# Input projection of a hybrid encoder layer: stick-breaking transposes and heads, statistics broadcast and convolution taps at other ticks

## Chip, cores, metric

One Trainium2 chip, one of its cores. The metric is the device time of one execution in microseconds; several executions are timed and the median is given. One further execution is profiled.

## What is computed

One layer (`DEPTH = 1`) over a sequence of 1024 rows of width 1024, all in float32. The projection `u` has 3328 columns and is split over three mixers; their outputs are concatenated, projected, and followed by an MLP with a squared ReLU.

```python
h = rms_norm(x, mix_norm_g)
u = einsum('btd,dc->btc', h, w_in)
sb_q, sb_k, sb_v, r_q, r_k, r_v, r_g, c_a, c_gate = split(u)
# 1. stick-breaking attention, 4 heads of 64, q and k normalised by head
z = q.k / sqrt(64);  mask: key < query
w = exp(log_sigmoid(z) + reverse_cumsum(log_sigmoid(-z), shifted));  y_sb = w @ v
# 2. retention, 8 heads of 64: rotary(q), rotary(k), decayed causal scores,
#    then rms_norm by head and silu(r_g) * ret
# 3. conformer convolution, 256 channels: (a + b) * sigmoid(gate + b),
#    31 causal depthwise taps, layer_norm over channels, silu
x = x + concat([y_sb, y_ret, y_conv]) @ w_out
x = x + relu(rms_norm(x) @ w_ff1)**2 @ w_ff2
```

## The kernel before

All float32 products are made of three passes: each operand is split into a high part (cast on ACT, lines 181 and 769) and a remainder (subtracted on DVE or POOL, lines 182 and 770), and `mm3` (lines 118 to 120) multiplies high by high, low by high and high by low.

**Order of the work.** The code is written out without loops on the chip. The input projection runs group by group of weight columns (`GROUPS`); each half of a tile (four of the eight 128-row pieces of the contraction) is one *tick*. `at_tick(t, order, fn)` hangs other work on a tick, and `tick` emits it, by `order`, ahead of that tick's matmuls. What is emitted is then arranged by a scheduler that works with a cost model of its own: the tick sets a priority and no fixed place, so an engine's instructions can stand earlier or later than their tick. Each engine then runs its own list strictly in order. In `conv_taps` a group of taps is tied behind an *anchor*, the latest evacuation of a projection tile on DVE (line 561 or 726).

**Ticks.** The first group (q and k of head pair 0, and all v) runs ahead of tick 0, over all eight PSUM banks. Ticks 0 to 15 are the group "qk1" (q and k of head pair 1, tiles of 256 columns, `gemm_narrow`); its tiles go into the two banks of tag "g" in turn, and a tile's bank comes free when `qk1_evac` has normalised it (`sb_norm`, lines 288 to 300). Ticks 16 to 31 are the convolution's two halves, gated by `conv_gate` (lines 498 to 509), which needs `rbc`, the row statistic broadcast over partitions (`row_bcast`, lines 249 to 256). Ticks 32 to 95 are the four wide retention groups, ticks 96 to 111 the first part of the output projection (`out_job(0, dt)`, three of eight contraction pieces); then `out_job(1, dt)` adds the other five.

**Stick-breaking.** `sb_norm` normalises a tile of q and k into `qn`, in a tile of tag "cv", of which there are two; two row tiles share one. `sb_turn` transposes four row tiles (lines 305 and 306) and splits them into `qs`, `ka`, `kb` (lines 314 to 321: per call 4 plus 2 ACT and 6 DVE operations). A head is 12 steps, four heads 48 steps; a step's `a_step` makes scores (lines 348 to 351, banks "z"), two sigmoids, a product scan on DVE (line 361) and a product on POOL (line 365); `b_step` transposes the weights two ticks later (line 376) and splits them (378, 379); `c_step` multiplies with v after each pair of steps (395).

**Pair 0 before the change.** `norm0(range(4))` runs ahead of tick 0; `turn0(0)` at tick 1 is followed by `norm0(range(4, 8))`, since both "cv" tiles are in use until the transposes; `turn0(1)` at tick 3. The 48 steps start at ticks 2 to 49. `row_bcast` is emitted at tick 16, with its own two "cv" tiles.

**Convolution.** 124 taps (line 588 for the first of a channel tile, 591 for the others; 31 taps, two channel tiles, two halves of the sequence, the second half first) run on DVE at ticks 35 to 99, `per` of them at a tick. A half's two `conv_norm_a` (transposes 601, statistics 606 to 608, scaling 612) and `conv_norm_b` (transposes 621, lines 626 to 629) follow; the results are split by `split_mixed(4)` and `split_mixed(5)` for `out_job(1, dt)`.

Of the kernel before, what the change touches and what calls it, by code (L numbers as in the profile page):

```python
# [15 lines left out]
P = 128  # L16
# [3 lines left out]
NT = T // P  # L20
# [58 lines left out]
def build(tc, d):  # L79
# [27 lines left out]
    def slot(tag, shape=(P, T), dt=F32):  # L107
        pool = xp if tag[0] == "x" else pg
        return pool.tile(list(shape), dt, tag=tag, name=nm(tag + "_"))

    def page(i, shape=(P, T), dt=F32):
        return slot(f"P{i}", shape, dt)

    def small(tag, shape, bufs=2, dt=F32):
        return sm.tile(list(shape), dt, tag=tag, name=nm(tag), bufs=bufs)
# [133 lines left out]
    def row_bcast(out, col, tag, by="cv"):  # L249
        for hf in range(2):  # L250
            ps = bank(tag)
            dg = small(by, (P, 4, P))
            V.tensor_tensor(out=dg, in0=ident.unsqueeze(1).to_broadcast([P, 4, P]),
                            in1=col[:, 4 * hf:4 * hf + 4].unsqueeze(2).to_broadcast([P, 4, P]), op=ALU.mult)
            TE.matmul(ps, ones, dg.rearrange("p a b -> p (a b)"), start=True, stop=True)
            S.copy(out[:, 512 * hf:512 * hf + 512], ps)
# [7 lines left out]
    def at_tick(t, order, fn):  # L264
        steps.setdefault(t, []).append((order, len(steps.get(t, [])), fn))
# [21 lines left out]
    def sb_norm(pair, tt, src):  # L287
        sq = small("e1", (P, 256))
        S.activation(sq, src, AF.Square)
        ss = small("ss", (P, 4))  # L290
        V.tensor_reduce(out=ss, in_=sq.rearrange("p (a b) -> p a b", b=DH), axis=AX.X, op=ALU.add)
        V.tensor_scalar(out=ss, in0=ss, scalar1=1.0 / DH, scalar2=ceps[:, tt:tt + 1], op0=ALU.mult, op1=ALU.add)
        rs = small("rs", (P, 4))
        rpow(rs, ss)
        if tt % 2 == 0:
            tb[tt // 2] = small("cv", (P, 2, 256))
        qn = tb[tt // 2][:, tt % 2, :]
        V.tensor_tensor(out=qn.rearrange("p (a b) -> p a b", b=DH), in0=src.rearrange("p (a b) -> p a b", b=DH),
                        in1=rs.unsqueeze(2).to_broadcast([P, 4, DH]), op=ALU.mult)

    def sb_turn(pair, tg):
        pq, pk = bank("t"), bank("t")
        for u in range(4):
            qn = tb[2 * tg + u // 2][:, u % 2, :]
            TE.transpose(pq[:, u * P:u * P + P], qn[:, 0:P], ident)
            TE.transpose(pk[:, u * P:u * P + P], qn[:, P:2 * P], ident)
        ts = slice(tg * 512, tg * 512 + 512)
        t = hd[pair]
        for e in range(2):
            a = slice(64 * e, 64 * e + 64)  # L310
            b = slice(64 * (1 - e), 64 * (1 - e) + 64)
            gq, gk = vec[a, V_GQ:V_GQ + 1], vec[a, V_GK:V_GK + 1]
            qs, ka, kb = t["qs", e], t["ka", e], t["kb", e]
            S.activation(qs[a, ts], pq[a, :], AF.Copy, scale=gq)
            V.scalar_tensor_tensor(out=qs[b, ts], in0=pq[a, :], scalar=gq, in1=qs[a, ts].bitcast(F32),  # L315
                                   op0=ALU.mult, op1=ALU.subtract)
            S.activation(kb[a, ts], pk[a, :], AF.Copy, scale=gk)
            V.scalar_tensor_tensor(out=kb[b, ts], in0=pk[a, :], scalar=gk, in1=kb[a, ts].bitcast(F32),
                                   op0=ALU.mult, op1=ALU.subtract)
            S.copy(ka[b, ts], kb[a, ts].bitcast(F32))  # L320
            V.tensor_copy(ka[a, ts], kb[b, ts].bitcast(F32))
# [9 lines left out]

    mix_sb = {}

    def sb_head(pair, e, t0):
        h = 2 * pair + e
        tick0 = t0
        for m in range(4):
            st = {"carry": {}, "first": True}

            def a_step(m, jg, ii, key, st):  # L340
                t = hd[pair]
                qs, ka, kb = t["qs", e], t["ka", e], t["kb", e]
                s0, i = 512 * jg, 2 * m + ii
                n = min(512, P * (i + 1) - s0)
                last = s0 + n == P * (i + 1)
                pz = bank("z")
                qt = qs[:, i * P:i * P + P]
                TE.matmul(pz[:, 0:n], qt, kb[:, s0:s0 + n], start=True, stop=False)
                if last:
                    TE.matmul(pz[:, n - P:n], identb, maskb, start=False, stop=False)  # L350
                TE.matmul(pz[:, 0:n], qt, ka[:, s0:s0 + n], start=False, stop=True)  # L351
                be = small("be", (P, 512), 3)
                kp = small("kp", (P, 513), 2)
                S.activation(kp[:, 0:n], pz[:, 0:n], AF.Sigmoid, scale=-0.125)  # L354
# [12 lines left out]

            def b_step(m, jg, ii, key, st):
                if ii == 0:
                    st["w", jg] = page(18, (P, 4, 2, P), F32R), page(19, (P, 4, 2, P), F32R)  # L370
                wth, wtl = st["w", jg]
                be, n = st["be", jg, ii]
                nj = n // P
                pt = bank("t")
                for j in range(nj):
                    TE.transpose(pt[:, j * P:j * P + P], be[:, j * P:j * P + P], ident)  # L376
                src = pt[:, 0:n].rearrange("p (j c) -> p j c", c=P)
                S.copy(wth[:, 0:nj, ii, :], src)
                V.tensor_tensor(out=wtl[:, 0:nj, ii, :], in0=src, in1=wth[:, 0:nj, ii, :].bitcast(F32),
                                op=ALU.subtract)  # L380
# [22 lines left out]

            for jg in range((2 * m + 1) // 4, -1, -1):
                for ii in range(2):
                    at_tick(t0, 30, lambda a=(m, jg, ii, None, st): a_step(*a))
                    at_tick(t0 + 2, 20, lambda a=(m, jg, ii, None, st): b_step(*a))
                    t0 += 1
                at_tick(t0 + 2, 10, lambda a=(m, jg, None, st): c_step(*a))
        return t0  # L410

    def parts(n, lo_engine=None):
# [54 lines left out]
    def norm0(tts):  # L467
        for tt in tts:
            sb_norm(0, tt, raw0[tt // 2][:, tt % 2, 0:256])

    def turn0(tg):
        sb_turn(0, tg)
        if tg == 0:
            norm0(range(4, 8))

    norm0(range(4))
    for tt in range(NT):
        v_evac(tt, raw0[tt // 2][:, tt % 2, 256:512])
    at_tick(1, 5, lambda: turn0(0))
    at_tick(3, 5, lambda: turn0(1))  # L480
    t1 = sb_head(0, 0, 2)
    t1 = sb_head(0, 1, t1)
    t1 = sb_head(1, 0, t1)
    sb_end = sb_head(1, 1, t1) + 4
    mix_sb[1] = page(17)
    sb_prepare(1)

# [3 lines left out]
            at_tick(now[0] + 1, 5, lambda: sb_turn(1, tt // 4))  # L491

    gemm_narrow(qk1_evac)
    rbc = slot("DM")
    at_tick(now[0], 6, lambda: row_bcast(rbc, rstd, "o"))
    glu = [None, None]

    def conv_gate(ct, hf, pa, pgt):
# [131 lines left out]

    c0 = 35
    taps = [(ct, hf, j) for hf in (1, 0) for j in range(TAPS) for ct in range(2)]
    per = [1] * 22 + [2] * 7 + [3] * 16 + [2] * 20
    n, t = 0, c0
    while n < len(taps):
        at_tick(t, 40, lambda a=taps[n:n + per[t - c0]]: conv_taps(a))
        n, t = n + per[t - c0], t + 1
    for t2, t in ((2, 81), (3, 85), (0, 100), (1, 102)):
        at_tick(t, 25, lambda t2=t2: conv_norm_a(t2))
        at_tick(t + 2, 25, lambda t2=t2: conv_norm_b(t2))  # L640

# [212 lines left out]
    def out_proj(pi, dt, hf):  # L854
        tsl = slice(512 * hf, 512 * hf + 512)
        w = taken[pi, dt]
        ps = bank("o" if pi else "g")
        for k in w:
            mm3(ps, w[k][0], w[k][1], mh[k][:, tsl], ml[k][:, tsl], k == min(w), k == max(w))
        V.tensor_tensor(out=x2[dt][:, tsl], in0=ps, in1=x2[dt][:, tsl], op=ALU.add)  # L860

    jobs = [(pi, dt) for pi in range(2) for dt in range(NK)]
# [329 lines left out]
```

## Time and profile before

| | us |
|---|---|
| median of 3 runs (1157.25 to 1157.94) | 1157.6 |
| the profiled execution, its own time | 1159.54 |
| its span, first to last instruction | 1157.8 |
| TensorE (PE) busy in the span | 1121.4 (97%) |
| VectorE (DVE) busy | 897.7 (78%) |
| ScalarE (ACT) busy | 484.1 (42%) |
| GpSimd (POOL) busy | 519.1 (45%) |
| mean granted TensorE clock, as a share of 2.4 GHz | 0.992 |

PE is the engine with the least idle time, so the time is read from the places where PE is idle or runs at the lower clock, and from what ended each idle time. The view of windows gives by stretch the busy time of each engine, with the number of instructions, and the granted clock; the view of waits says which instruction of which engine ended the idle time before an instruction; the timeline lists instructions in order of time.

### The profile page before, as it was taken

The numbers are of one execution on the slowest core, as the hardware profiler recorded it, in microseconds if no ns is written. First come the engines' busy times: TensorE is split into PE (matmuls) and PEld (weight loads), VectorE is DVE, ScalarE is ACT, GpSimd is POOL, SyncE is SP. The second block draws the span as 40 slices with busy tenths as digits, with TensorE's granted clock in tenths as the row PEclk, the third lists the DMA queues.
The fourth block names the chain that finished last, engine by engine and source line by source line (L and its number), as shares of the span: only waits on it lengthen the run. The fifth ranks groups of instructions, "written<-read, shape, count | busy, mean of one in ns | idle before, by whom it ended". The sixth has DMA issues, their size and how long they took to land.

```text
span 1157.8 us, 15678 instructions
## 1 busy us (share of the span) xinstructions
PE 1121.4 (97%) x5416; PEld 933.0 (81%) x5416; DVE 897.7 (78%) x1378; ACT 484.1 (42%) x917; POOL 519.1 (45%) x413
## 2 busy tenths in 40 slices
PE   8968899999999989999999999999999999999997
PEld 6857788888887878888888888888878788888886
DVE  7498677787899898579975666666699897886963
ACT  7366655453322242356433333333443443444441
POOL 4356234473555463242466565655583531522300
PEclk9989999999999989999999999999999999999999
DMA  8101011030202051112254444444787464552342
GB/s 277 48 1 46 19 42 55 19 110 15 87 24 87 20 217 61 55 73 91 78 187 148 152 161 140 164 146 141 279 304 264 130 219 129 164 182 82 110 136 73
DMA packets 63727, 137.00 MB, mean 118 GB/s; under 512 B 7200, under 2 KB 11936, under 8 KB 63648
## 3 DMA queue, kind: packets, MB, share of 16 engines
q1 hardware_dynamic: 63072, 135.56, 35.3%
q8 instruction: 43, 0.70, 0.3%
q10 hardware_dynamic: 576, 0.44, 0.1%
q14 instruction: 36, 0.29, 0.1%
HBM read 98.22 MB, written 37.75 MB: 117 GB/s over the span
## 4 chain that ended last, share of the span: by engine, by line
PE 47%; DVE 5%; issue 3%; POOL 2%; ACT 0%; DVEq 0%; POOLq 0%; ACTq 0%
PE g L119 4%; PE g L120 4%; PE g L118 4%; PE t L119 4%; PE t L118 4%; PE t L120 4%; PE o L119 4%; PE o L120 4%; PE o L118 4%; PE z L119 4%; PE z L118 4%; PE z L120 4%; DVE wlo L182 1%; POOL sum L903 1%; POOL wr L903 0%
## 5 line engine op out<-in xcount | busy, mean ns | idle before, releaser
L182 DVE TENSOR_TENSOR wlo<-sum,whi 128x512 fp32r<-128x512 f32 x78 | 80.2, 1029 | 84.2 <-ACT whi L181 84.1
L181 ACT CAST whi<-sum 128x512 fp32r<-128x512 f32 x78 | 47.9, 617 | 101.4 <-POOL sum L903 50.9
L182 DVE TENSOR_TENSOR wlo<-wr,whi 128x512 fp32r<-128x512 f32 x80 | 76.4, 960 | 6.9 <-ACT whi L181 6.9
L908 POOL TENSOR_TENSOR sum<-wr 128x512 f32<-128x512 f32 x16 | 23.4, 1466 | 120.2 <-DMA wr<-in_w_ff_dram 92.7
L365 POOL TENSOR_TENSOR be<-be,kp 128x512 f32<-128x512 f32 (+3 forms) x48 | 44.6, 932 | 70.5 <-DVE kp L361 33.1
L181 ACT CAST whi<-wr 128x512 fp32r<-128x512 f32 x80 | 48.2, 620 | 51.7 <-PE t L119 17.6
L196 POOL TENSOR_TENSOR rs<-ss,nhalf 128x4 f32<-128x4 f32 (+1 forms) x36 | 36.8, 1024 | 66.8 <-DVE ss L699 44.7
L361 DVE TENSOR_TENSOR_SCAN kp<-kp 128x512 f32<-128x512 f32 (+3 forms) x48 | 53.4, 1118 | 10.1 <-ACT kp L354 9.8
L591 DVE SCALAR_TENSOR_TENSOR DM__439_2052<-glu,vec,DM__439_2052 128x512 f32<-128x512 f32 x60 | 52.7, 921 | 0.0
L591 DVE SCALAR_TENSOR_TENSOR glu<-glu,vec 128x512 f32<-128x512 f32 x60 | 50.3, 881 | 0.0
L354 ACT ACTIVATE kp<-z 128x512 f32<-128x512 f32 (+3 forms) x48 | 23.7, 493 | 36.2 <-PE z L351 22.0
L182 POOL TENSOR_TENSOR wlo<-wraw,whi 128x512 fp32r<-128x512 f32 x18 | 28.4, 1585 | 22.6 <-ACT whi L181 21.2
L903 POOL TENSOR_TENSOR sum<-wr,sum 128x512 f32<-128x512 f32 x19 | 32.8, 1725 | 9.9 <-DVE wlo L182 9.9
L903 POOL TENSOR_TENSOR sum<-sum,wr 128x512 f32<-128x512 f32 x18 | 24.4, 1357 | 12.5 <-DVE wlo L182 12.5
L376 PE MATMUL t<-ident,be 128*128 128x128 f32 x144 | 25.1, 276 | 4.2 <-DVE P__108_534 L315 1.6
L181 ACT CAST whi<-wraw 128x512 fp32r<-128x512 f32 x33 | 20.1, 619 | 19.5 <-PE g L119 10.0
L563 POOL TENSOR_TENSOR P__538_2584<-P__397_1882 128x128 f32<-128x128 f32 x16 | 14.5, 906 | 29.0 <-DVE P__397_1882 L561 29.0
L182 POOL TENSOR_TENSOR wlo<-rawq,whi 128x512 fp32r<-128x512 f32 x14 | 23.7, 1699 | 7.8 <-ACT whi L181 7.5
L355 ACT ACTIVATE be<-z 128x512 f32<-128x512 f32 (+3 forms) x48 | 23.7, 493 | 8.4 <-PE t L376 8.4
L376 PEld LDWEIGHTS t<-ident,be 128*128 128x128 f32 x144 | 16.9, 140 | 8.1 <-issue 5.7
L903 POOL TENSOR_TENSOR wr<-wr,wr 128x512 f32<-128x512 f32 x16 | 22.5, 1406 | 1.1
L681 ACT ACTIVATE e<-o 128x256 f32<-128x256 f32 x16 | 6.2, 385 | 38.6 <-PE o L679 37.9
(2941 smaller groups left out, 4141.6 us busy)
## 6 DMA issues: line engine op xcount, KB each, us to landing
wr<-in_w_ff_dram SPq DMA_DIRECT2D x40, 512.0 KB, 3.9
wraw<-in_w_in_dram SPq DMA_DIRECT2D x32, 256.0 KB, 2.7
rawq<-in_w_in_dram SPq DMA_DIRECT2D x20, 256.0 KB, 2.8
P__396_1881<-in_rot_dram SPq DMA_DIRECT2D x32, 128.0 KB, 2.0
wraw<-in_w_out_dram SPq DMA_DIRECT2D x10, 256.0 KB, 2.8
rawq<-in_w_out_dram SPq DMA_DIRECT2D x6, 256.0 KB, 3.5
P__18_144<-in_xT_dram SPq DMA_DIRECT2D x1, 512.0 KB, 5.1
P__24_182<-in_xT_dram SPq DMA_DIRECT2D x1, 512.0 KB, 6.2
```

Of the source, the lines that this page charges most:

```text
L118: TE.matmul(out, lh, rh, start=start, stop=False, skip_group_check=on)
L119: TE.matmul(out, lh, rl, start=False, stop=False, skip_group_check=on)
L120: TE.matmul(out, ll, rh, start=False, stop=stop, skip_group_check=on)
L181: S.copy(hi, raw)
L182: (lo_engine or GP).tensor_tensor(out=lo, in0=raw, in1=hi.bitcast(F32), op=ALU.subtract)
L196: GP.tensor_tensor(out=out, in0=in_, in1=nhalf[:, 0:in_.shape[1]], op=ALU.pow)
L354: S.activation(kp[:, 0:n], pz[:, 0:n], AF.Sigmoid, scale=-0.125)
L361: V.tensor_tensor_scan(rev, rev, rev, kp[:, n:n + 1], op0=ALU.mult, op1=ALU.bypass)
L365: GP.tensor_tensor(out=be[:, 0:n], in0=be[:, 0:n], in1=kp[:, 1:n + 1], op=ALU.mult)
L376: TE.transpose(pt[:, j * P:j * P + P], be[:, j * P:j * P + P], ident)
L591: V.scalar_tensor_tensor(out=acc, in0=src, scalar=vec[:, o:o + 1], in1=acc, op0=ALU.mult, op1=ALU.add)
L903: (eng or GP).tensor_tensor(out=o, in0=x, in1=y, op=ALU.subtract)
```

## The change

Six things are altered, all of them order or storage; every product, tap and norm stays.

1. `norm0` runs for all eight row tiles ahead of tick 0; its results lie in pages 19 and 10 and no longer in "cv" tiles. `turn0(0)` moves from tick 1 to 3, `turn0(1)` from 3 to 6.
2. The 48 steps start at the ticks of `sb_ticks`: ten steps at ticks 6 to 15, twenty at ticks 16 to 30 (two at each third tick), the rest from tick 31.
3. `row_bcast` for `rbc` is emitted ahead of tick 0, with pages 10 and 11 for its operand.
4. Taps by tick: 15 ticks of one (35 to 49), 14 of two (50 to 63), 16 of three (64 to 79), 16 of one and two in turn (80 to 95), nine of one (96 to 104).
5. The norms of the second half go from ticks 81 and 85 to 72 and 76, those of the first half from 100 and 102 to 105 and 107 (`conv_norm_b` two ticks later each).
6. `split_mixed(4)` is emitted with `split_mixed(5)` after the seventh output job and no longer after the sixth, and `out_job(1, dt)` takes its pieces in the order 3, 6, 7, 4, 5.

```diff
-            dg = small(by, (P, 4, P))
+            dg = small(by, (P, 4, P)) if by else page(10 + hf, (P, 4, P))
...
         if tt % 2 == 0:
-            tb[tt // 2] = small("cv", (P, 2, 256))
-        qn = tb[tt // 2][:, tt % 2, :]
+            if pair == 0:
+                tb[0, tt // 2] = nrm0[tt // 4][:, tt % 4:tt % 4 + 2, :]
+            else:
+                tb[1, tt // 2] = small("cv", (P, 2, 256))
+        qn = tb[pair, tt // 2][:, tt % 2, :]
...
+    sb_ticks = list(range(6, 16)) + [16 + 3 * (i // 4) + (0, 0, 1, 2)[i % 4] for i in range(20)] + list(range(31, 60))
...
-                    at_tick(t0, 30, lambda a=(m, jg, ii, None, st): a_step(*a))
-                    at_tick(t0 + 2, 20, lambda a=(m, jg, ii, None, st): b_step(*a))
+                    at_tick(sb_ticks[t0], 30, lambda a=(m, jg, ii, None, st): a_step(*a))
+                    at_tick(sb_ticks[t0] + 2, 20, lambda a=(m, jg, ii, None, st): b_step(*a))
...
-        if tg == 0:
-            norm0(range(4, 8))
-
-    norm0(range(4))
+
+    rbc = slot("DM")
+    row_bcast(rbc, rstd, "o", None)
+    nrm0 = [page(19, (P, 4, 256)), page(10, (P, 4, 256))]
+    norm0(range(NT))
...
-    at_tick(1, 5, lambda: turn0(0))
-    at_tick(3, 5, lambda: turn0(1))
-    t1 = sb_head(0, 0, 2)
+    at_tick(3, 5, lambda: turn0(0))
+    at_tick(6, 5, lambda: turn0(1))
+    t1 = sb_head(0, 0, 0)
...
-    rbc = slot("DM")
-    at_tick(now[0], 6, lambda: row_bcast(rbc, rstd, "o"))
...
-    per = [1] * 22 + [2] * 7 + [3] * 16 + [2] * 20
+    per = [1] * 15 + [2] * 14 + [3] * 16 + [1, 2] * 8 + [1] * 9
...
-    for t2, t in ((2, 81), (3, 85), (0, 100), (1, 102)):
+    for t2, t in ((2, 72), (3, 76), (0, 105), (1, 107)):
...
-        for k in w:
-            mm3(ps, w[k][0], w[k][1], mh[k][:, tsl], ml[k][:, tsl], k == min(w), k == max(w))
+        ks = (3, 6, 7, 4, 5) if pi else tuple(w)
+        for k in ks:
+            mm3(ps, w[k][0], w[k][1], mh[k][:, tsl], ml[k][:, tsl], k == ks[0], k == ks[-1])
...
-        if dt in (1, 5, 6):
-            split_mixed({1: 3, 5: 4, 6: 5}[dt])
+        if dt == 1:
+            split_mixed(3)
+        if dt == 6:
+            split_mixed(4)
+            split_mixed(5)
```

## Rows read from the trace of the kernel before

**Rows 1.** Windows by stage: length, each engine's busy us (xinstructions), PE clock, DMA share, GB/s.

```profile
57.70:72.23 14.53, 7.23 (x31) 5.12 (x30) 13.77 (x38) 10.59 (x23) 8.49 (x9) 0.69 0.00 0
72.23:104.79 32.56, 27.45 (x211) 25.53 (x209) 28.35 (x61) 21.89 (x47) 16.30 (x16) 0.98 0.02 5
104.79:178.35 73.56, 70.43 (x385) 58.14 (x386) 51.30 (x98) 40.58 (x89) 29.71 (x30) 1.00 0.16 47
...
248.49:307.79 59.30, 59.30 (x353) 51.69 (x352) 45.62 (x88) 21.12 (x53) 26.45 (x28) 1.00 0.13 43
307.79:361.11 53.32, 52.57 (x272) 44.39 (x270) 52.71 (x92) 12.05 (x29) 28.16 (x28) 1.00 0.14 45
361.11:420.00 58.89, 56.97 (x311) 47.83 (x310) 52.83 (x97) 19.26 (x46) 30.59 (x31) 1.00 0.20 64
420.00:440.00 20.00, 16.20 (x75) 13.42 (x75) 19.91 (x37) 5.16 (x13) 12.30 (x11) 0.83 0.82 315
...
480.00:500.00 20.00, 19.78 (x88) 16.04 (x87) 11.03 (x14) 8.12 (x12) 5.52 (x4) 1.00 0.24 79
```

**Rows 2.** Windows of 5 us in the first and seventh of these stages, columns as above.

```profile
65.00:70.00 5.00, 3.20 (x13) 2.69 (x14) 4.78 (x13) 4.51 (x9) 2.03 (x2) 0.50 0.00 0
...
430.00:435.00 5.00, 5.00 (x18) 4.32 (x18) 4.95 (x12) 0.75 (x2) 2.68 (x3) 0.50 1.02 401
```

**Rows 3.** Waits of PE, 50 to 110 us: total us, times, longest.

```profile
PE z L348 <- DVE P__71_449 L318: 3.5, 1, 3.5
PE t L305 <- DVE cv L298: 3.0, 3, 1.9
PE g L118 <- DVE cv L298: 2.2, 2, 1.1
```

**Rows 4.** Timeline of PE: last matmul of tick 3, first of tick 4 (start, us).

```profile
57.68 0.29 PE L120 MATMUL g<-whi,xl__59_380 128*128 128x256 f32 x1
...
72.23 0.41 PE L118 MATMUL g<-whi,xh__12_101 128*128 128x256 f32 x1
```

**Rows 5.** Timeline of DVE, the first normalisation of a tick's tile.

```profile
71.45 0.42 DVE L298 TENSOR_TENSOR cv<-g,rs 128x256 f32<-128x256 f32 x1
```

**Rows 6.** Lines of DVE, 57.7 to 104.8 us: xcount, busy us, mean ns.

```profile
L361 DVE TENSOR_TENSOR_SCAN kp<-kp 128x512 f32<-128x512 f32 (+3 forms) x11 | 11.8, 1077 | 1.8 <-ACT kp L354 1.7
```

**Rows 7.** Views of single lines: xcount, duration ns min/median/max, first and last start.

```profile
L253 DVE TENSOR_TENSOR cv<-ident,rstd x2: 694/706/719, 124.1 to 125.7; 128x512 f32<-128x512 f32 x2
...
L255 PE MATMUL o<-cv,ones x4: 592/630/697, 124.9 to 127.0; 128*128 128x512 f32 x4
...
L591 DVE SCALAR_TENSOR_TENSOR glu<-glu,vec x60: 710/742/1778, 343.2 to 443.8; 128x512 f32<-128x512 f32 x60
...
L606 DVE BATCH_NORM_STATS2 bst<-t x8: 406/418/432, 367.5 to 470.8; 128x6 f32<-128x256 f32 x8
...
L612 DVE TENSOR_SCALAR cv<-t,bmv,rs x8: 535/537/544, 373.1 to 472.9; 128x256 f32<-128x256 f32 x8
...
L628 DVE TENSOR_SCALAR e<-t,vec x8: 532/540/544, 377.7 to 479.4; 128x256 f32<-128x256 f32 x8
...
L601 PE MATMUL t<-ident,DM__439_2052 x8: 270/272/275, 349.6 to 387.2; 128*128 128x128 f32 x8
```

**Rows 8.** Line 770 on DVE, 410 to 440 us, as above.

```profile
L770 DVE TENSOR_TENSOR xl__795_4303<-P__542_2591,xh__794_4302 x2: 677/678/679, 420.3 to 422.6; 128x512 fp32r<-128x512 f32 x2
L770 DVE TENSOR_TENSOR xl__827_4465<-P__543_2592,xh__826_4464 x2: 1743/1750/1756, 423.8 to 425.5; 128x512 fp32r<-128x512 f32 x2
```

**Rows 9.** Waits of PE, 360 to 440 us: the longest.

```profile
PE o L678 <- DVE P__396_1881 L695: 3.1, 1, 3.1
```

**Rows 10.** Timeline of POOL beside the splits of rows 8.

```profile
423.71 4.61 POOL L182 TENSOR_TENSOR wlo<-wraw,whi 128x512 fp32r<-128x512 f32 x3 [1.61 <-ACT whi L181]
```

**Rows 11.** Timeline of PE: first transposes of the last norms, and the wait on their last split.

```profile
455.68 0.60 PE L601 MATMUL t<-ident,glu 128*128 128x128 f32 x4
...
483.23 0.50 PE L119 MATMUL o<-P__880_4699,whi 128*128 128x512 f32 x1 [0.22 <-DVE P__880_4699 L770]
```

More of the change, by code (lines that the diff above doesn't have):

```diff
@@ L303, in sb_turn @@
         for u in range(4):
-            qn = tb[2 * tg + u // 2][:, u % 2, :]
+            qn = tb[pair, 2 * tg + u // 2][:, u % 2, :]
             TE.transpose(pq[:, u * P:u * P + P], qn[:, 0:P], ident)
@@ L332, in build @@
     mix_sb = {}
+    sb_ticks = list(range(6, 16)) + [16 + 3 * (i // 4) + (0, 0, 1, 2)[i % 4] for i in range(20)] + list(range(31, 60))
     def sb_head(pair, e, t0):
         h = 2 * pair + e
-        tick0 = t0
         for m in range(4):
@@ L405, in sb_head @@
                 for ii in range(2):
-                    at_tick(t0, 30, lambda a=(m, jg, ii, None, st): a_step(*a))
-                    at_tick(t0 + 2, 20, lambda a=(m, jg, ii, None, st): b_step(*a))
+                    at_tick(sb_ticks[t0], 30, lambda a=(m, jg, ii, None, st): a_step(*a))
+                    at_tick(sb_ticks[t0] + 2, 20, lambda a=(m, jg, ii, None, st): b_step(*a))
                     t0 += 1
-                at_tick(t0 + 2, 10, lambda a=(m, jg, None, st): c_step(*a))
+                at_tick(sb_ticks[t0] + 2, 10, lambda a=(m, jg, None, st): c_step(*a))
         return t0
@@ L472, in turn0 @@
         sb_turn(0, tg)
-        if tg == 0:
-            norm0(range(4, 8))
-    norm0(range(4))
+    rbc = slot("DM")
+    row_bcast(rbc, rstd, "o", None)
+    nrm0 = [page(19, (P, 4, 256)), page(10, (P, 4, 256))]
+    norm0(range(NT))
     for tt in range(NT):
         v_evac(tt, raw0[tt // 2][:, tt % 2, 256:512])
-    at_tick(1, 5, lambda: turn0(0))
-    at_tick(3, 5, lambda: turn0(1))
-    t1 = sb_head(0, 0, 2)
+    at_tick(3, 5, lambda: turn0(0))
+    at_tick(6, 5, lambda: turn0(1))
+    t1 = sb_head(0, 0, 0)
     t1 = sb_head(0, 1, t1)
     t1 = sb_head(1, 0, t1)
-    sb_end = sb_head(1, 1, t1) + 4
+    sb_head(1, 1, t1)
     mix_sb[1] = page(17)
```

## The prediction

> **What bounds the kernel now.** I read the page first: PE is busy for 97% of the span, so a change of order can win only where PE is idle or runs at its lower clock. Then the windows by stage show where that is [rows 1]. Between 57.7 and 72.2 us (from the end of tick 3 to tick 4) PE is busy for 7.23 of 14.53 us, 7.3 idle; in ticks 4 to 15 for 27.45 of 32.56, 5.1 idle; in ticks 16 to 31 3.1 of 73.6 are idle; in ticks 80 to 95 1.9 of 58.9; at the passage into the output projection (420 to 440) 3.8 of 20. Beside that the granted clock falls in two places, to 0.50 of 2.4 GHz, which is its lower level of 1.2 GHz [rows 2]. At 0.69 over 14.53 us it was low for 0.31 / 0.5 x 14.53 = 9 us, at 0.83 over 20 for 6.8 us; PE was at work in an estimated 6.5 us of each (3.2 and 5.0 in the rows shown, the rest beside them), and half of that, about 3.3 us, is what each fall cost. Everything after 500 us is untouched by the change.
>
> The waits name what ended PE's idle time [rows 3]: the transposes wait for a normalised tile (3.0 us), the first scores for the split of the transposed tile (3.5), the projection for a bank that the normalisation has not yet left (2.2). The timeline shows the knot. After tick 3 both "g" banks are full; tick 4 needs the first to be normalised; that result wants a "cv" tile, and both hold pair 0 until `turn0(0)` and then `turn0(1)` have transposed them. The bank's normalisation comes at 71.45 us [rows 5], and tick 4 starts at 72.23, 14.3 us behind the end of tick 3 [rows 4].
>
> But what is DVE doing meanwhile? It is busy for 13.77 of 14.53 us, and for 28.35 of 32.56 in the next stage [rows 1]: 42.1 of 47.1, or 89%. So the knot of "cv" tiles orders a queue that is full anyway; untying it frees little unless DVE's own work leaves the stage.
>
> **The change, part by part.**
>
> *Norms into pages, transposes at ticks 3 and 6, heads from tick 6 (ticks 4 to 15).* The same normalisations and transposes run on the same engines, so they cost what they cost. What leaves the stage is four of the fourteen steps that started by tick 15. Each takes off DVE a scan of 1.08 us [rows 6], a split of a transposed tile (0.68 for 512 columns by the same kind of subtraction [rows 8], about 0.5 at a mean of 350 columns), and about 0.2 of small copies: 4 x 1.78 = 7.1 us. The broadcast enters with two products of 0.71 us [rows 7], 1.4. Net -5.7 us on the engine that sets the pace, so tick 16 comes about 5.7 us earlier, near 99 us. From below: 0, if the order of ACT or POOL takes DVE's place. From above: if every wait goes, 12.4 us idle and 3.3 of clock. I take 5.7, because the DVE share of 89% leaves only 5 us more.
>
> *Broadcast behind the first group.* PE's four pieces of 0.63 us [rows 7] now fall where PE waits for tick 4 in any case, so 2.5 us leave ticks 16 to 31. The new wait is for the row statistic, and on PE the gemm of ticks 0 to 3 or the idle time behind it is queued there; if the scheduler puts the broadcast ahead of those ticks, they merely fill the idle time later. I cost it at nothing; without that cover it would be the pieces' 2.5 us and as much for the product ahead of them.
>
> *Twenty steps instead of sixteen in ticks 16 to 31.* PE has 70.4 us of work there [rows 1]; four steps add about 0.9 each (two score products, two to four transposes, the share of `c_step`), 3.6, less the 2.5 of the broadcast: 71.5. DVE has 51.3 + 7.1 - 1.4 = 57, so it fits behind PE. Of the 3.1 us idle I leave 2: at the doubled ticks two steps want the two "z" banks and the two tiles of the scan at once. That is 73.5, as before, and the gain at tick 16 is kept: -5.7.
>
> How long a scan takes is not one number here: taps, which like it read two SBUF tensors, go from 0.71 to 1.78 us [rows 7]. The Trainium skill, "SBUF — State Buffer", section "Who interferes with whom", says that a VectorE instruction with two SBUF inputs and a GpSimd instruction that reads SBUF exclude each other, the second waiting for the whole of the first. That speaks against pushing steps closer together, since every scan is followed by a POOL product: by the rule the four moved scans could take some 4 us more on DVE. The spread in the taps agrees with it. The sum stays, as DVE has 16 us to spare in that stage.
>
> *Taps and norms of the second half (ticks 48 to 95).* Seven taps move to ticks 50 to 56, where DVE is busy for 45.6 of 59.3 us [rows 1]: covered. Ticks 80 to 95 lose eight taps of 0.74 and two pairs of norms, each 2 x (0.42 + 0.54 + 0.54) = 3.0 us on DVE [rows 7]: 11.9 of 52.8 us. PE's 1.9 us idle there should go. But the norms' 6.0 us land in ticks 72 to 79, in a stage where DVE has no room (52.7 of 53.3). The cover is the second "g" bank, two ticks or 24 matmuls of 19.78 / 88 = 0.225 us [rows 1], 5.4 us; I charge 0.5. Net -1.5, from -2.7 (the 0.8 us of ticks 64 to 79 gone as well) to +4 (all of the 6.0 on PE, less 1.9).
>
> *The passage at 420 to 440 us.* The longest wait, 3.1 us, is for line 695 [rows 9], which stood on DVE behind eight splits of line 770. They take 0.68 us, but 1.75 beside the POOL splits of the weights [rows 8, 10]. They start when the last projection tick lets go of the operands' storage, which the change leaves as it is, and no tap lies among them. So I take 0, and -7 (3.8 idle and 3.3 clock) as the bound should the order fall differently.
>
> *Tail of the convolution.* The last norms are planned five ticks later; at 9 matmuls of 0.225 in an output tick that is at least 10 us. Before, the first of them began at 455.7 and the last split came at 483.2, with PE waiting 0.2 us for it [rows 11]: 27.5 us for operations that add up to less than half of that. Taking pieces 6 and 7 ahead moves the need back by six matmuls, 1.35 us, and the other half of the sequence gives some cover. With the retention work gone from these ticks the operations can follow faster; I charge 0.5, from 0 to +15 (below).
>
> **Sum:** -5.7 + 0 - 1.5 + 0 + 0.5 = -6.7 us. The profiled execution took 1159.54, so it would take 1152.8; the median lies 1.9 lower, at 1157.6, and goes to 1150.9.
>
> **Rivals.**
>
> *The passage clears too.* With three taps fewer between ticks 90 and 95 the eight splits and line 695 stand in another order, or the splits meet no POOL work and take 8 x 0.68 = 5.4 us, not 10. Then PE's 3.1 us wait and the stretch at 1.2 GHz go: 6 us more, 1145. For it: half of the splits' time is contention. Against: the storage that releases them is untouched. The Trainium skill, "TensorE: Matmul & The Clock Gate", section "What's actually happening", says that idleness throttles PE and activity releases it; the fall to 0.50 behind the wait in [rows 2] agrees, and by that rule the gain would exceed the wait itself.
>
> *It doesn't do what it says.* Ticks only set priorities: the first transposes of line 601, planned for tick 81, ran at 349.6 us [rows 7], well ahead of tick 80 at 361. If the scheduler places the heads and norms much as before, or DVE's queue gives the gain back in ticks 16 to 31, nothing changes: 1157 to 1158.
>
> *The tail comes late (slower).* If the chain of the last norms keeps its 27.5 us and starts as far behind its tick as before, it starts near 455.7 + 10.2 + 5 us and ends near 498. PE enters the second part near 481 (the wait at 483.2 lies some ten matmuls into it) and has work for 24 more, 5.4 us, until 486: the other half of the first job, and pieces 3, 6, 7. It would wait 12 us, and at 1.2 GHz lose some 3 more: +15 - 0.5, so 1165. It decides from the point where the last split comes more than some 7 us later than PE's work ends. For it: five ticks later by plan. Against: the chain was long because it ran beside the last retention chunks.
>
> **How the numbers follow.** Two runs differ by up to 0.06% from the median here, and about 0.2% (2.3 us) is what a measurement can tell from no change. Forecast (1147 to 1155): 0.50; the passage clears or the first stage wins more (1139 to 1147): 0.20; no change (1155.3 to 1159.9): 0.15; slower by the tail or by new waits at the doubled ticks: 0.15. So faster 0.70, same 0.15, slower 0.15. The predicted time is 1151. The range takes in both gains and no change, from 1140 to 1160.
>
> **What would show it.** Right: tick 16 near 99 us and tick 32 near 172 (178.35 before); DVE over 90% busy until tick 16 and PE still idle for some 6 us ahead of tick 4; no PE wait over 0.5 us between 361 and 415; the wait for line 695 still there. Wrong: PE idle time in ticks 16 to 31 above 5 us, waits on banks in ticks 72 to 80, or a wait of several us for a split of piece 4 or 5 near 485.

## The result and the profile after

| | before | after |
|---|---|---|
| median (before: 4 runs, after: 4 runs, 1167.73 to 1169.35) | 1157.77 | 1168.82 |
| ratio, with its 95% interval | | 1.0092 [1.0074, 1.0109] |
| the profiled execution | 1159.54 | 1169.35 |
| its span | 1157.8 | 1167.6 |
| PE busy | 1121.4 | 1125.4 |
| mean granted clock | 0.992 | 0.988 |

The change makes the kernel 11.1 us slower. The forecast was 1151, with a range from 1140 to 1160: the time lies outside it and on the other side.

The lines of the code after stand 3 to 5 further down: line 182 is unchanged, taps 591 are 595, the norm's lines 601, 606, 612 and 628 are 605, 610, 616 and 632, the projection's evacuation 559 and 561 is 563 and 565, retention's 658 and 711 are 660 and 715, the splits 769 and 770 are 773 and 774.

The windows of after by stage, cut where its own ticks begin (ticks 4, 16, 80 and 94 start at 74.17, 99.96, 361.38 and 424.59 us), with the columns of [rows 1]:

```profile
58.73:74.17 15.44, 8.38 (x34) 5.61 (x33) 13.98 (x40) 11.32 (x25) 9.36 (x9) 0.71 0.00 0
74.17:99.96 25.79, 22.71 (x178) 21.75 (x177) 20.57 (x44) 15.38 (x34) 12.06 (x13) 0.98 0.02 3
99.96:165.04 65.08, 63.34 (x339) 53.08 (x340) 43.38 (x83) 35.88 (x75) 26.61 (x26) 1.00 0.15 45
303.75:361.38 57.63, 55.78 (x286) 47.06 (x284) 56.11 (x102) 13.29 (x33) 30.80 (x31) 0.97 0.13 40
361.38:424.59 63.21, 56.05 (x303) 47.16 (x302) 45.18 (x86) 15.19 (x41) 27.83 (x29) 0.97 0.15 42
425.00:445.00 20.00, 15.31 (x87) 13.28 (x87) 19.37 (x27) 10.63 (x24) 13.32 (x11) 0.91 0.90 341
480.00:500.00 20.00, 16.36 (x70) 12.69 (x69) 11.13 (x22) 5.33 (x10) 4.04 (x5) 0.91 0.04 14
```

The early ticks are faster, as forecast: tick 16 starts at 99.96 us, 4.8 earlier than before. By tick 80 nothing of that is left (361.38 against 361.11). Ticks 80 to 94 then leave PE idle for 63.21 - 56.05 = 7.2 us, where [rows 1] had 1.9 between 361 and 420; and the output jobs at 480 to 500 us have 3.6 idle, where it was 0.2.

The waits of PE between 300 and 520 us in after (total us, times, longest):

```profile
PE z L671 <- DVE P__545_2613 L672: 3.9, 1, 3.9
PE g L119 <- DVE wlo L182: 3.9, 2, 2.2
PE o L118 <- ACT xh__875_4690 L773: 2.9, 1, 2.9
PE t L660 <- DVE e L632: 2.4, 1, 2.4
PE t L715 <- POOL e L710: 1.8, 1, 1.8
```

Only one of the five has a counterpart before: the passage into the output projection, where [rows 9] waits for line 695 and after waits for 672, which stands behind the same splits. The other four are new (for line 182 there was one wait of 0.4 us before), and the runs below tie them to three edits: 1.8 us in ticks 68 and 69 (taps), 3.9 and 2.4 in ticks 80 to 84 (norms), 2.9 near 494 us (tail).

### The profile page after: what moved, and what is told of

Its sections match the earlier page's. It is cut to its first block, busy times and chain, and to the rows that moved or that the text cites. A ratio compares the mean times of both kernels' runs of the same rounds, so it can differ in the third digit from the quotient of the medians.

```text
span 1167.6 us, 15654 instructions
## 1 busy us (share of the span) xinstructions
PE 1125.4 (96%) x5416; PEld 938.2 (80%) x5416; DVE 899.3 (77%) x1378; ACT 483.4 (41%) x917; POOL 525.8 (45%) x413
## 4 chain that ended last, share of the span: by engine, by line
PE 81%; DVE 10%; issue 3%; DMA 3%; POOL 2%; ACT 1%; SPq 0%; POOLq 0%; DVEq 0%; ACTq 0%
PE g L118 11%; PE g L119 11%; PE g L120 10%; PE t L120 5%; PE o L119 5%; PE t L118 5%; PE t L119 5%; PE o L118 5%; PE o L120 5%; PE z L118 4%; PE z L119 4%; PE z L120 4%; DVE glu L595 2%; PE o L400 1%; DVE DM__444_2079 L595 1%
## 5 line engine op out<-in xcount | busy, mean ns | idle before, releaser
L196 POOL TENSOR_TENSOR rs<-ss,nhalf 128x4 f32<-128x4 f32 (+1 forms) x36 | 39.3, 1095 | 77.0 <-DVE ss L703 49.0
L595 DVE SCALAR_TENSOR_TENSOR glu<-glu,vec 128x512 f32<-128x512 f32 x60 | 52.9, 919 | 0.0
L671 PE MATMUL z<-P__543_2611,P__544_2612 128*128 128x128 f32 x128 | 18.1, 285 | 3.9 <-DVE P__545_2613 L672 3.9
L181 ACT CAST whi<-rawq 128x512 fp32r<-128x512 f32 x23 | 14.2, 620 | 17.3 <-issue 8.3
```

The source lines that it names most:

```text
L181: S.copy(hi, raw)
L196: GP.tensor_tensor(out=out, in0=in_, in1=nhalf[:, 0:in_.shape[1]], op=ALU.pow)
L595: V.scalar_tensor_tensor(out=acc, in0=src, scalar=vec[:, o:o + 1], in1=acc, op0=ALU.mult, op1=ALU.add)
```

## The experiments

The theory after the result was: the edits to taps, norms and tail (4, 5, 6 in the section on the change) cost more than the first three gain, and the cost is DVE's. The rivals were that the first three lose their gain by themselves, that the order of the pieces in the output jobs does it, and that it is the passage. The runs compare with the kernel before on the same chip (medians 1158.3 to 1158.6); e1 to e4 ran on one chip, e5 to e8 on a second, e9 to e12 on a third. The intervals of two ratios overlap where medians lie some 3 us apart or less; a difference of that size is told only where a trace shows its place.

| run | edits | median us | ratio to before |
|---|---|---|---|
| e1 | 1, 2, 3 | 1152.5 | 0.9956 [0.9937, 0.9975] |
| e2 | 4, 5, 6 | 1168.2 | 1.0079 [1.0062, 1.0096] |
| e3 | all, norms of the second half late as before | 1160.3 | 1.0018 [1.0007, 1.003] |
| e4 | all but the taps | 1166.2 | 1.0066 [1.005, 1.0081] |
| e5 | all, fewer taps in ticks 71 to 79 | 1159.5 | 1.001 [1.0, 1.002] |
| e6 | e1 and the order of pieces | 1154.6 | 0.9969 [0.9956, 0.9982] |
| e7 | e1 and the whole tail | 1157.4 | 0.9999 [0.9989, 1.0009] |
| e8 | e1 and the earlier taps | 1155.3 | 0.9975 [0.9959, 0.9992] |
| e9 | e1, one step at a tick | 1152.85 | 0.9945 [0.9925, 0.9964] |
| e10 | the step ticks alone | 1157.5 | 0.9993 [0.9979, 1.0007] |
| e11 | e1, an early split | 1155.6 | 0.9972 [0.9958, 0.9985] |
| e12 | e1, weights split on DVE | 1154.8 | 0.9957 [0.9941, 0.9972] |

**e1: the stick-breaking edits alone.** After, with taps, norms and tail as before:

```diff
-    per = [1] * 15 + [2] * 14 + [3] * 16 + [1, 2] * 8 + [1] * 9
+    per = [1] * 22 + [2] * 7 + [3] * 16 + [2] * 20
-    for t2, t in ((2, 72), (3, 76), (0, 105), (1, 107)):
+    for t2, t in ((2, 81), (3, 85), (0, 100), (1, 102)):
...
```

> Only parts 1 to 3 of the change: norms of pair 0 in pages, transposes and steps at the new ticks, early broadcast; taps, norms of the convolution and the order of the output pieces as before. Theory A (the loss comes from the taps, the convolution's norms and the tail, and the stick-breaking part wins what its ticks show, 4 to 6 us by tick 64): 1151 to 1154 us, no PE wait of 2 us between 360 and 385 and none on a split of piece 4 or 5 near 490. Theory B (the time won early is given back, since DVE in ticks 64 to 95 cannot follow a PE that comes sooner): 1157 to 1162, with the waits of the changed kernel at 366 to 381 still there.

1152.5, 6 us faster than before (by the interval 2.9 to 7.3). Tick 16 starts at 99.98 and tick 80 at 357.06. The traces show 4.4 us of the gain: line 245, the statistic of the MLP's norm, which stands behind all of the altered work, starts at 545.3 us (before: 549.7). The spans of the two profiled executions differ by 3.4 us more behind it, where no edit reaches. What after loses, it loses with edits 4 to 6 put on top of e1.

**e2: taps, norms and tail alone.** The kernel before with edits 4, 5 and 6.

> Only parts 4 to 6: new taps by tick, new ticks of the convolution's norms, new order of the pieces and of splits 4 and 5; the stick-breaking part as before. Theory A: 1170 to 1176, that is the changed kernel's time plus the 4 to 6 us that the stick-breaking part wins. Theory B: about as before, 1156 to 1160, since nothing comes sooner.

1168.2, 9.6 us slower than before, a little below what theory A wanted. In after the same three edits cost 16.3 us on top of e1. So the parts don't simply add up: beside edits 4 to 6 the gain of e1 is gone. In e2 ticks 80 to 89 take 40.75 us (before 39.2, after 44.8), PE waits at most 0.3 us at a time for a remainder of line 182, and not at all for line 628 (632 in after): the early norms, so costly in after, leave little trace there without edits 1 to 3. Of the 9.8 us by which e2 is late at line 245, 6.2 come behind tick 90: the passage holds a wait of 6.6 us for a product on POOL (line 706), and the tail waits as in after. Why the same edits meet other waits there was not separated further.

**e3: the norms late again.** After, but with `((2, 81), (3, 85), (0, 105), (1, 107))`.

> The changed kernel with the norms of the second half back at ticks 81 and 85, all else as changed. If these norms, set among three taps a tick, are what holds up the weight splits on DVE (PE waits of 2.2 and 1.7 us for line 182 near 367): 1161 to 1164, those waits gone. If the taps by tick or the tail carry the loss: 1167 to 1170, as changed.

1160.3, 8.5 us faster than after. Ticks 80 to 89 take 38.4 us, and PE's waits for lines 182 and 632 are gone; of the 8.5 us, 44.8 - 38.4 = 6.4 lie in those ten ticks. Beside the other edits, the early norms are the largest single loss.

**e4: the taps of before.** After, with `per = [1] * 22 + [2] * 7 + [3] * 16 + [2] * 20`. In this kernel the norms of one tile at tick 72 stand ahead of its last two taps, so that they work on the sum without these two, and the kernel's output is not the layer's; the number of operations is the same, so that its time can still be read.

> The changed kernel with the old taps by tick (ticks 35 to 99), the new ticks of the norms and the new order of the pieces. If the taps by tick carry the loss: 1158 to 1162. If norms and tail carry it: 1167 to 1172, a little slower than changed, because the second half's last tap then lies at tick 72, the very tick of its first norm.

1166.2: against e7, which differs by the norms alone, 8.8 us. So early norms cost about the same with either list of taps, and the earlier taps are not what makes them dear.

**e5: early norms, fewer taps beside them.** After, with fewer taps where the norms now stand and the rest behind them:

```diff
-    per = [1] * 15 + [2] * 14 + [3] * 16 + [1, 2] * 8 + [1] * 9
+    per = [1] * 15 + [2] * 14 + [3] * 7 + [1] * 9 + [2] * 24 + [3]
```

> The changed kernel with the norms of the second half at ticks 72 and 76 as changed, but one tap a tick instead of three in ticks 71 to 79 (18 taps of some 0.74 us fewer on DVE there); the taps left out run later, two a tick in ticks 80 to 103, the last at 104. If the norms lose time because DVE has no room there: ticks 80 to 90 take 39 to 41 us as before (44.8 in the changed kernel), no wait for a weight split of line 182 over 1 us between 361 and 385, in all 1162 to 1165 (the tail's loss stays). If it is the place of their transposes in PE's order, whatever DVE has to do: the wait for line 632 stays and ticks 80 to 90 take 44 us or more, 1167 to 1170.

1159.5, 9.3 us faster than after, with the norms still at 72 and 76. Ticks 80 to 89 take 36.1 us, less than in any other of these kernels. All that PE waits for between 355 and 410 us in e5:

```profile
PE g L118 <- DVE P__403_1908 L565: 0.9, 1, 0.9
```

So a norm at tick 72 does no harm by its tick alone; it harms where DVE has three taps at each tick beside it. (With other taps the scheduler also lays out PE's list in another order, see below.) The timeline shows what the norms push away. DVE in after, around the start of tick 80 at 361.38 (start, us, line, operation, count):

```profile
357.08 2.28 DVE L595 SCALAR_TENSOR_TENSOR glu<-glu,vec 128x512 f32<-128x512 f32 x2
359.29 1.00 DVE L154 TENSOR_TENSOR ww<-wraw,ww 128x512 fp32r<-128x512 f32 x1
360.21 3.48 DVE L595 SCALAR_TENSOR_TENSOR glu<-glu,vec 128x512 f32<-128x512 f32 x2
363.61 0.75 DVE L610 BATCH_NORM_STATS2 bst<-t 128x6 f32<-128x256 f32 x2
...
365.39 1.21 DVE L182 TENSOR_TENSOR wlo<-rawq,whi 128x512 fp32r<-128x512 f32 x1
366.52 1.77 DVE L595 SCALAR_TENSOR_TENSOR glu<-glu,vec 128x512 f32<-128x512 f32 x1
...
368.37 1.59 DVE L182 TENSOR_TENSOR wlo<-wraw,whi 128x512 fp32r<-128x512 f32 x1
369.88 0.47 DVE L563 SCALAR_TENSOR_TENSOR P__403_1908<-g,rstd,P__402_1907 128x256 f32<-128x256 f32 x1
```

And PE, for which the last bracket is the idle time and what ended it; the last line is DVE's, ahead of PE's third wait:

```profile
366.65 0.50 PE L119 MATMUL g<-wlo,xh__40_265 128*128 128x512 f32 x1 [2.17 <-DVE wlo L182]
...
370.01 0.50 PE L119 MATMUL g<-wlo,xh__52_341 128*128 128x512 f32 x1 [1.70 <-DVE wlo L182]
...
376.89 0.60 PE L625 MATMUL t<-ident,cv 128*128 128x128 f32 x4
...
380.13 0.41 PE L660 MATMUL t<-ident,P__398_1903 128*128 128x128 f32 x2 [2.42 <-DVE e L632]
381.41 0.50 PE L118 MATMUL g<-whi,xh__12_101 128*128 128x512 f32 x1 [0.87 <-DVE P__403_1908 L565]
...
378.21 0.54 DVE L632 TENSOR_SCALAR e<-t,vec 128x256 f32<-128x256 f32 x1 [2.53 <-ACT e L630]
```

Three things come late, two of them behind one full queue. The remainders of the next group's weights (line 182) keep PE waiting twice, since the product with `wlo` stands next in PE's list. The evacuation at 369.88 comes 8.5 us behind the start of tick 80; in e1 it comes at 361.88, 4.8 behind 357.06. PE hardly waits for it, as it has just lost 3.9 us to the remainders. The third, 2.42 us, is not DVE's queue: the second norm's transposes (line 625) start at 376.89 behind the matmuls of a tick and hold banks of tag "t" until ACT (line 630) and DVE (line 632) have read them in turns, while retention's transposes (660) stand next in PE's list and want the same tag. DVE sat idle for 2.53 us in between. In e5 line 632 comes later still behind its transposes (364.73 and 371.41) and PE doesn't wait, as the second pair of line 660 stands in PE's list only at 374.01. So this wait hangs on the order of PE's list. (In e4 it is 5.0 us, and there line 632 does stand behind six taps, 4.05 us.)

**e6: the order of the pieces.** e1 with `ks = (3, 6, 7, 4, 5)` for the second output jobs.

> The kernel with the stick-breaking part alone (1152.5), and the order 3, 6, 7, 4, 5 of the output pieces; taps, norms and splits as before. If the order of the pieces is harmless: 1151.5 to 1153.5, the wait of 0.2 us for the last split of piece 5 gone. If it is what makes the tail lose: 1156 or more, with a wait on pieces 6 or 7 near 475.

1154.6, between the two forecasts, with an interval of the ratio that overlaps that of e1. No cost is shown for it.

**e7: the tail.** e1 with the late norms of the first half, the joint split and the order of pieces.

> The stick-breaking part alone, with the first half's norms at ticks 105 and 107, split 4 beside split 5, and the new order of the pieces; taps and the second half's norms as before. If the later norms are the tail's loss: 1156 to 1159, with a PE wait of 2.5 to 3 us for the cast of piece 4 (line 773) and the lower clock behind it, as in the changed kernel. If the tail was late only because the taps ended late: 1152 to 1154.

1157.4, 4.9 us more than e1, and clear of it by the intervals. PE in e7, and then in after, where the output job reaches the first of the late pieces:

```profile
485.60 0.73 PE L118 MATMUL o<-xh__875_4690,whi 128*128 128x512 f32 x2 [2.75 <-ACT xh__875_4690 L773]
486.81 0.50 PE L119 MATMUL o<-xl__876_4691,whi 128*128 128x512 f32 x1 [0.47 <-DVE xl__876_4691 L774]
```

```profile
494.31 0.73 PE L118 MATMUL o<-xh__875_4690,whi 128*128 128x512 f32 x2 [2.85 <-ACT xh__875_4690 L773]
495.52 0.80 PE L119 MATMUL o<-xl__876_4691,whi 128*128 128x512 f32 x1 [0.48 <-DVE xl__876_4691 L774]
```

Where [rows 11] waited 0.22 us, both wait 2.75 or 2.85 and 0.47 or 0.48, and in both the granted clock of 480 to 500 us is 0.91 where it was 1.00. Some 2 us of e7's loss may not be the tail's: its waits in the passage add up to 6.0 us, as in e11, against 2.8 in e1. The chain of the last norms in after, by two single lines (count, duration in ns, first and last start): its first transposes start at 472.4 us and its last product at 494.2, just ahead of the split that PE waits for:

```profile
L605 PEld LDWEIGHTS t<-ident,glu x8: 139/142/143, 472.4 to 482.0; 128*128 128x128 f32 x8
...
L633 POOL TENSOR_TENSOR glu<-e,e x4: 722/736/743, 483.7 to 494.2; 128x256 f32<-128x256 f32 x4
```

The chain waits above all for PE, not for DVE, which is busy for 14.2 of the 22.6 us from 472.4 to 495. A norm scaled by line 616 is transposed by line 625 only when PE's list comes to it, 4.0 us later for the first tile and 3.0 for the second:

```profile
476.15 1.00 DVE L616 TENSOR_SCALAR cv<-t,bmv,rs 128x256 f32<-128x256 f32 x2 [0.26 <-POOL rs L196]
...
481.12 0.27 PE L625 MATMUL t<-ident,cv 128*128 128x128 f32 x1
...
486.84 0.99 DVE L616 TENSOR_SCALAR cv<-t,bmv,rs 128x256 f32<-128x256 f32 x2 [0.59 <-POOL rs L196]
...
490.86 0.60 PE L625 MATMUL t<-ident,cv 128*128 128x128 f32 x4
```

**e8: the earlier taps.** e1 with the taps at other ticks only:

```diff
-    per = [1] * 22 + [2] * 7 + [3] * 16 + [2] * 20
+    per = [1] * 15 + [2] * 14 + [3] * 16 + [2] * 13 + [1] * 7
```

> The stick-breaking part alone with the changed taps up to tick 79 and 33 taps in ticks 80 to 99 (two a tick, then one), norms, splits and piece order as before. If moving seven taps ahead is worth what DVE gets free: 1149 to 1152, less PE idle time at 365 to 375. If the two taps a tick in ticks 50 to 56 cost what ticks 66 to 70 show in the changed kernel (a wait of 1.8 us for the product of line 710): 1154 to 1156, with that wait.

1155.3, 2.8 us more than e1. The intervals overlap, as for e6, so the times alone don't show a cost; the traces do. The loss stands at one place: ticks 68 and 69 take 11.5 to 12.0 us in the four kernels with edits 1 to 3 and the early taps (after, e3, e5, e8) and 8.4 in the six with edits 1 to 3 and the taps of before (e1, e4, e6, e7, e11, e12). In e8 tick 70 starts at 330.43 (e1: 327.25). In e2, without edits 1 to 3, the early taps cost nothing there (7.0 us, as before). In e8 PE waits for retention's transposes, and the clock between 320 and 340 us is 0.91 (e1: 1.00). PE in e8:

```profile
326.51 0.44 PE L715 MATMUL t<-ident,e 128*128 128x128 f32 x2 [1.84 <-POOL e L710]
```

DVE in e8, and then the same operations in e1:

```profile
315.20 2.55 DVE L595 SCALAR_TENSOR_TENSOR DM__444_2079<-glu,vec,DM__444_2079 128x512 f32<-128x512 f32 x3
317.67 0.40 DVE L702 TENSOR_REDUCE ss<-e 128x4 f32<-128x256 f32 x1
...
323.88 0.41 DVE L707 TENSOR_TENSOR e<-o,rs 128x256 f32<-128x256 f32 x1
```

```profile
315.04 0.40 DVE L702 TENSOR_REDUCE ss<-e 128x4 f32<-128x256 f32 x1
315.37 1.76 DVE L595 SCALAR_TENSOR_TENSOR DM__444_2079<-glu,vec,DM__444_2079 128x512 f32<-128x512 f32 x2
...
319.71 0.41 DVE L707 TENSOR_TENSOR e<-o,rs 128x256 f32<-128x256 f32 x1
```

In e8 three taps stand ahead of the reduction of line 702, which comes 2.6 us later, and 707 behind it 4.2 us later; it feeds the product 710 on POOL and so PE's transposes, 715. At ticks 64 to 79 both lists have three taps a tick: these are no more in number, they stand further ahead in the queue.

**e9 and e10: which of the first three edits gains.** e9 is e1 with `sb_ticks = list(range(4, 60))`, one step at a tick from tick 4; e10 is the kernel before with the new `sb_ticks` and nothing else.

> The stick-breaking part alone (norms in pages, transposes at 3 and 6, early broadcast), but the 48 steps one a tick from tick 4, with no doubled ticks: two steps fewer leave the first stage than with the new list. If the gain comes from DVE work leaving ticks 4 to 15 (four steps, 5.7 us by the prediction): tick 16 near 102, in all 1154 to 1156. If it comes from the pages that replace the two cv tiles: as with the new list, 1151.5 to 1153.5, tick 16 near 100.

> The kernel before with the new list of step ticks alone; the norms stay in cv tiles, the transposes at ticks 1 and 3, the broadcast at tick 16. If DVE's work is what holds the first stage: 1152 to 1154, tick 16 near 100 as with the whole part. If the cv tiles hold it: 1156 to 1158, tick 16 at 103 or later, tick 4 still near 72.

e9 keeps the gain (1152.85), e10 has none that can be measured (1157.5). The windows 45 to 105 and 105 to 178 us, of before, of e9 and of e10:

```profile
45.00:105.00 60.00, 47.59 (x326) 42.63 (x326) 48.69 (x112) 39.18 (x84) 28.61 (x28) 0.91 0.01 4
105.00:178.00 73.00, 69.87 (x384) 57.65 (x384) 50.93 (x97) 40.05 (x87) 29.50 (x30) 1.00 0.16 47
```

```profile
45.00:105.00 60.00, 50.19 (x337) 44.37 (x336) 48.42 (x113) 40.15 (x85) 30.54 (x28) 0.91 0.01 3
105.00:178.00 73.00, 71.46 (x396) 60.62 (x395) 52.19 (x97) 38.19 (x85) 31.65 (x29) 1.00 0.20 59
```

```profile
45.00:105.00 60.00, 49.58 (x330) 44.53 (x329) 45.59 (x107) 35.82 (x77) 30.48 (x29) 0.91 0.06 16
105.00:178.00 73.00, 69.86 (x386) 57.82 (x385) 51.73 (x97) 41.13 (x89) 25.51 (x26) 1.00 0.15 48
```

In the first window PE's idle time of 12.4 us falls by 2.6 in e9 and 2.0 in e10. In the second it falls from 3.1 to 1.5 in e9, where the broadcast has left these ticks, and stays at 3.1 in e10, where it has not; PE's waits for the broadcast's product (line 255) are 1.1 us in before and 1.5 in e10 there, and e9 and e1 have none. In e9 DVE is as busy in the first window as before (48.42 and 48.69 us), so it isn't less work on DVE that shortens PE's waits. And yet tick 16 starts at 98.07 in e10, 6.7 us earlier than before, and at 103.19 in e9, only 1.6 earlier. The start of a tick tells what was put off, not what was gained: the steps that e10 defers fall due later, and its lead of 6.7 us has shrunk to 1.95 at tick 80 (e9: 4.4; e1: 4.05) and to 1.0 at line 245 (e9: 4.2; e1: 4.4). Whether the pages or the early broadcast gain was not measured apart.

**e11 and e12: the passage.** e11 emits `split_mixed(0)` at tick 57; e12 takes the weights' remainders of the first output jobs on DVE and no longer on POOL:

```diff
-        return {k: w_quarter(GP if pi == 0 else V) for k in ks}
+        return {k: w_quarter(V) for k in ks}
```

> The stick-breaking part alone, with the split of piece 0 (two of the eight subtractions of line 770 at the passage into the output projection) emitted at tick 57, where DVE has room. If the queue of splits on DVE sets PE's wait at the passage: 2 to 4 us faster, 1148.5 to 1151, PE's waits between 415 and 445 under 1.5 us in all. If the passage is bound otherwise (the storage that the last tick releases, or POOL's weight splits): 1152 to 1153, waits as before.

> The stick-breaking part alone, with the low parts of the first output weights (line 182, six tiles of 128x512) on DVE instead of POOL. If POOL's splits are what stretches the DVE subtractions from 0.68 to 1.75 us: all eight of line 770 at 0.7, and the passage shorter by 0 to 3 us, 1150 to 1152.5. If DVE's queue matters more than the contention: 1153 to 1156, with longer waits of PE on DVE between 415 and 445.

Neither beats e1 (1155.6 and 1154.8). In e11 the edit put nothing elsewhere: the two subtractions of piece 0 start at 264.1 and 264.9 us, as they do in e1 (264.3 and 265.1), so they never were among those at the passage, and neither forecast was tested. Even so it is 2.2 us behind e1 at line 245 (547.5), with other waits in the passage: 3.9 us for line 565 and 2.1 for line 699. In e12 the price of the splits fell as planned. Line 774 on DVE in e1, then in e12 (duration in ns: min/median/max, first and last start):

```profile
L774 DVE TENSOR_TENSOR xl__791_4297<-P__121_573,xh__790_4296 x2: 1201/1480/1760, 413.9 to 415.1; 128x512 fp32r<-128x512 f32 x2
L774 DVE TENSOR_TENSOR xl__825_4463<-P__548_2619,xh__824_4462 x2: 674/1214/1755, 420.2 to 420.8; 128x512 fp32r<-128x512 f32 x2
```

```profile
L774 DVE TENSOR_TENSOR xl__791_4297<-P__121_573,xh__790_4296 x2: 677/677/677, 417.0 to 417.6; 128x512 fp32r<-128x512 f32 x2
L774 DVE TENSOR_TENSOR xl__825_4463<-P__548_2619,xh__824_4462 x2: 673/674/674, 420.6 to 421.2; 128x512 fp32r<-128x512 f32 x2
```

The Trainium skill, "SBUF — State Buffer", section "Who interferes with whom", lets a DVE instruction with two SBUF inputs and a POOL instruction that reads SBUF exclude each other. The runs agree: with POOL's splits gone from these microseconds, the same subtractions drop from up to 1.76 to 0.68 us. But the wait moves on instead of going: PE in e12, 405 to 450 us:

```profile
PE g L118 <- DVE P__403_1908 L565: 5.7, 1, 5.7
PE o L682 <- DVE P__402_1907 L699: 0.2, 1, 0.2
```

The passage's waits add up to 3.8 us before, 2.8 in e1 and 5.9 in e12, and the longest differs: line 695 before (699 in e1), 672 in after, 565 in e3, e11 and e12, a product on POOL in e2. What most of these waits are for stands somewhere in a full DVE queue, and the order of that queue changes with every edit; which rule of the scheduler sets it was not tested.

**The sum.** e1 (1152.5) + 2.8 (e8) + 4.9 (e7) = 1160.2, and e3, which has the same tail and, up to tick 79, the same taps, took 1160.3. That it fits so closely is luck, as each of these terms is uncertain by some 2 us. With the early norms, 8.5, it is 1168.8; but that term is itself after less e3, and so no test. A count that needs no medians takes the starts of the same marks in two traces (us):

| | tick 68 | tick 70 | tick 80 | tick 90 | line 245 |
|---|---|---|---|---|---|
| e1 | 318.87 | 327.25 | 357.06 | 396.92 | 545.3 |
| after | 318.97 | 330.45 | 361.38 | 406.18 | 561.4 |
| after less e1 | 0.1 | 3.2 | 4.3 | 9.3 | 16.1 |

By it 4.2 us are lost in ticks 68 to 79, 4.9 in ticks 80 to 89 and 6.8 behind them, so the whole is as by the medians and the shares are known to 2 to 4 us. The fastest kernels are e1 and e9, which leave out edits 4 to 6: about 0.5% faster than before, 1.4% faster than after.

## Why the prediction failed, step by step

**First stage (-5.7 + 0 + 0): near in size, wrong in its reason.** e1 gained 6 by the medians and 4.4 by the traces. Tick 16 came where the forecast wanted it (99.96, forecast near 99), and tick 32 even earlier (165.04, forecast near 172). PE's idle time ahead of tick 4 stayed, 15.44 - 8.38 = 7.1 us, as forecast (some 6); DVE, forecast over 90% busy until tick 16, was so for 34.6 of 41.2 us, 84%. But the step ascribed the gain to four steps that leave the stage, and e10 does just that and gains nothing that can be measured. So the size came out by luck. The sentence "untying it frees little unless DVE's own work leaves the stage" fell: e9 unties the tiles and moves the broadcast, with DVE as busy in the first window as before, and has the whole gain. The broadcast's leaving was counted as 2.5 us of PE's work, spent on the added steps; it also took away some 1.5 us of PE's idle time in ticks 16 to 31; the 2.0 to 2.6 us in the first window come with either edit. (`sb_ticks` puts 21 steps into ticks 16 to 31, and the prediction counted twenty; no run shows that it mattered.) A mark by tick (tick 16 near 99) was the wrong test, since deferral moves it by itself.

**Taps and norms of the second half (-1.5, bounds -2.7 to +4): the step that failed.** It measured +8.5 for the norms and +2.8 for the taps, 11.3 us and so 12.8 off (9.1 in ticks 68 to 89 by the traces). It had seen that the norms land in "a stage where DVE has no room" (52.7 of 53.3), and took the second "g" bank, 5.4 us, as cover for their 6.0. That cover holds for the evacuation alone, which came 8.5 us behind its tick. The weights' remainders stand in the same DVE queue and have no such cover, and the "t" banks are held by the norms while retention wants them; the prediction named neither. (Its 1.9 less 0.5 is 1.4 and not 1.5, a slip without weight.) Then the clock: PE waits of 2.42 and 0.87 us ahead of 381.4 are followed by matmuls that, from 382.7 us, start 0.43 us apart where they started 0.23 apart, at 0.97 over the 63 us of ticks 80 to 94. The upper bound of +4 left out the uncovered waits and the clock. "Covered" was also wrong for the seven taps: DVE had the time, but a tap ahead of line 702 delays a chain that PE needs. Why both cost much less without edits 1 to 3 (e2) stays open; the order of DVE's and PE's lists differs there.

**The loss of DVE work in ticks 80 to 95 ("PE's 1.9 us idle there should go").** DVE did become lighter (45.18 of 63.21 us, before 52.83 of 58.89), and PE's idle time rose to 7.2. An engine's mean load over fifteen ticks says nothing on the three at their start, where DVE was busy without a gap from 361 to 371 us.

**The passage (0).** Right on its face: no gain. But it was not the wait it had kept: PE's waits from 405 to 450 us were 5.3 us in after (3.9 for line 672, 0.8 and 0.6) against 3.8, and the lower clock was shorter (0.91 over 20 us, before 0.83). That the two about cancel is luck.

**Tail (+0.5, bounds 0 to +15).** Mis-sized: +4.9. The rival "the tail comes late" had the right mechanism and place (a wait for a split of piece 4 or 5), and the wrong price. It assumed a chain of 27.5 us; after's took 22, from 472.4 to 494.2. With the retention chunks gone the chain was faster, as the step hoped, but not by enough, for it stood 7.0 us in PE's own list: 2.85 + 0.48 us of waiting, and a stretch at the lower clock.

**The signs that were named.** "Waits on banks in ticks 72 to 80" and "a wait of several us for a split of piece 4 or 5" were two of the three signs of a failure, and both came, a little later than named: in ticks 80 to 84 and at 494 us. No PE wait over 0.5 us between 361 and 415 was the sign of success; there were four.

## What to carry to other kernels

When work is moved to another place in a full queue, list everything that stands behind it on that engine there and ask of each item which buffer covers it; the one that the bound engine needs next and that nothing covers (here the weights' remainders) sets the price. Judge a reordering by the idle time of the bound engine (here PE) up to a point where the same work is done in both, not by when a labelled step starts. If an edit has parts that touch different stages, measure them apart, and together: here one half was worth 6 us by itself, and the other cost 10 by itself and 16 on top of the first.

## What the runs showed of the hardware

A wait of PE was not always followed by the lower clock. In after a wait of 1.84 us at 327 us was, at 0.91 over 320 to 340 us, and so were 2.42 and 0.87 close together near 380; but 2.17 and 1.70 us at 366.65 and 370.01 were not: the matmuls behind them start 0.23 us apart. At 0.91 over 20 us the clock was at its lower level, 1.2 GHz, for 0.09 / 0.5 x 20 = 3.6 us, which by an estimate cost PE half of that, 1.8 us. So of two waits of about the same length one cost double. The tail shows it with one and the same wait: in after, 2.85 us ahead of 494.31, the clock over 480 to 500 us is 0.91; in e2 it is 1.00 there and over 500 to 520 as well, behind this wait:

```profile
493.80 0.73 PE L118 MATMUL o<-xh__877_4692,whi 128*128 128x512 f32 x2 [2.85 <-ACT xh__877_4692 L769]
```

What tells them apart was not tested.
